# Strassen's products with adding DMAs in the feed-forwards of a two-block model

## The chip, the cores and the metric

The kernel runs on one NeuronCore of a Trainium2 chip. The metric is device time in microseconds; the median of three runs of the kernel before is 2211.48 us (2207.61 to 2212.41). TensorE (PE) multiplies, VectorE (DVE) and ScalarE (ACT) work elementwise, GpSimd (POOL) helps with small things, and SyncE (SP) issues the DMAs.

## What is computed

256 tokens of width 1024 pass through two layers of one block and two of another. Each layer has a feed-forward, a mixer and a second feed-forward, so there are eight feed-forwards of one form, and only these are changed:

```
def swiglu(x, w13, w2):            # x: 256 x 1024, w13: 1024 x 5632, w2: 2816 x 1024
    a, b = jnp.split(x @ w13, 2, axis=-1)
    return (jax.nn.silu(a) * b) @ w2

x = layer_norm(ALPHA * x + 0.5 * swiglu(x, ...), g, b)      # first block
x = x + 0.5 * rms_norm(swiglu(rms_norm(x, g0), ...), g1)    # second block
```

All is float32. The mixers (gated recurrences, attention, convolutions) are as before.

## The kernel before

The tokens are two halves of 128, i = 0 and 1. A product is made of float32r parts: each operand is split into a rounded part (hi, wh, xh) and the rest (lo, wl, xl), and `mm3` (L301) adds hi*hi, hi*lo and lo*hi into PSUM, three matmuls with 512 columns moving for each 128 rows of the weights.

All weights come as one stream of 128x1024 tiles of 512 KB, the units, in the order in which they are used. `fetch` (L226) has SP load them into one of four stages, `split` makes the two parts: ACT copies a half into wh (L267), DVE subtracts it into wl (L273). `run_all` keeps the splits some units ahead of the matmuls (2 to 5), and the fetches four units ahead of the splits (STAGES).

A feed-forward has 11 groups of 256 hidden columns. A group takes four units, whose 512 columns are 256 of a and 256 of b. The first two groups (OWN) are done for each half of the tokens by itself, the others by `joint` for both halves at once: 12 matmuls to a unit, 48 to a group. `hidden` makes silu(a)*b of a group (L400, L402, L405); two steps later it is transposed (L285) and split (L410, L411), and it is then what stands in front of w2: `rows` and `joint` multiply 22 units of w2, each 128 x 1024, into two PSUM banks for each half ("big" in the trace, 12 matmuls for a unit). The table `FFN` gives the order: groups, and between them 8 and 8 units of w2; the last six (LAST) are done by each half for itself. Then comes the norm of that half, whose output `to_x` (L308, L309) transposes and splits into xh and xl.

A scheduler orders PE, ACT and DVE by a cost model; SP and GpSimd keep the order of the program. The code for a stage "s" (PRODUCTS, NEEDS, `operand`) is there but no entry of `FFN` calls it.

Of the kernel before, what the change touches and what calls it, by code (L numbers as in the profile page):

```python
# [19 lines left out]
P = 128  # L20
# [55 lines left out]
class Core:  # L76
# [5 lines left out]
    def __init__(self, ctx, tc, a, out, order):  # L82
        self.tc, self.nc, self.a, self.out = tc, tc.nc, a, out
        self.order = order
        p = lambda n, b, **k: ctx.enter_context(tc.tile_pool(name=n, bufs=b, **k))
        self.cp = p("cp", 1)
        self.stg = p("stg", STAGES)
        self.whp = p("whp", 2 * RING)
        self.sp = p("sp", SLOTS)
        self.vp = p("vp", 2)  # L90
        self.st = p("st", 12)
        self.big = p("big", 4, space=PSUM)
        self.grp = p("grp", 4, space=PSUM)

        self.phase, self.made = [], []
        ffn = _ffn_units()
        for what, _ in order:
            mixer = ("mixer1", 56) if what == "b1" else ("mixer2", 36)
            for kind, made in (("ffn", ffn), (mixer[0], [None] * mixer[1]), ("ffn", ffn)):
                self.phase += [(kind, m) for m in range(len(made))]  # L100
                self.made += made
        self.nunit = len(self.made)
        self.raw, self.next_raw = {}, 0
# [48 lines left out]
    def run_all(self):  # L152
# [3 lines left out]
        def part(i, h):  # L156
            hi, lo = (t[:, i, 512 * h:512 * h + 512] for t in (self.xh, self.xl))
            self.pin(self.nc.scalar.activation(hi, self.xT0[i][h], AF.Copy))
            self.pin(self.nc.vector.tensor_sub(lo, self.xT0[i][h], hi))
# [39 lines left out]
    def lead(self):  # L199


        kind, n = self.phase[min(self.pos[0], self.nunit - 1)]
        left = dict(ffn=len(_ffn_units()), mixer1=56, mixer2=36)[kind] - n
        if self.made[min(self.pos[0] + PAIR, self.nunit - 1)]:
            return PAIR
        return LEAD + (MORE if n < FIRST else max(0, MORE - left // RAMP))

    def paired(self):
        return int(self.made[min(self.next_split, self.nunit - 1)] is not None)
# [5 lines left out]
    def fetch(self, v):  # L215
        while self.next_dma <= min(v, self.nunit - 1):
            made = self.made[self.next_dma]
            if made is None:
                t = self.stages[self.next_dma] = self.stg.tile([P, 1024], F32, tag="stg", name=self.nm("stg"))
            elif made[0] in NEEDS:  # L220
                t = self.raw[NEEDS[made[0]], made[1]] = self.whp.tile([P, 1024], F32, tag="w", name=self.nm("raw"))
            else:
                t = None
            if t is not None:
                for c in (slice(0, 512), slice(512, 1024)) if self.next_raw == 0 else (slice(0, 1024),):
                    self.nc.sync.dma_start(t[:, c], self.a["ws"][self.next_raw][:, c])  # L226
                self.next_raw += 1
            self.next_dma += 1

    def operand(self, p, u):  # L230


        raw, add = self.raw, self.nc.vector.tensor_add
        if p == "p1":
            return raw["11", u]
        if p == "q5":
            t = raw.pop(("11", u))
            add(t, t, raw["12", u])
            raw["t1", u] = t
            return t  # L240
        if p == "p6":
            t = raw["t2", u] = self.whp.tile([P, 1024], F32, tag="w", name=self.nm("sum"))
            add(t, raw.pop(("t1", u)), raw["22", u])
            return t
        if p == "p3":
            return raw["22", u]
        if p == "p7":
            t = raw.pop(("12", u))
            add(t, t, raw.pop(("22", u)))
            return t  # L250
        if p == "p2":
            return raw["21", u]
        t = raw.pop(("t2", u))
        add(t, t, raw.pop(("21", u)))
        return t

    def split(self, u):
        while self.next_split <= min(u, self.nunit - 1):
# [3 lines left out]
            w = self.stages.pop(v) if made is None else self.operand(*made)  # L262
# [3 lines left out]
            for h, c in enumerate(halves if made is None else [slice(0, 1024)]):  # L266
# [8 lines left out]
            self.next_split += 1  # L275
            self.fetch(v + STAGES)
# [26 lines left out]
    def to_x(self, i, srcs):  # L303

        for h, src in enumerate(srcs):
            tp = self.transposed(src)
            hi, lo = (t[:, i, 512 * h:512 * h + 512] for t in (self.xh, self.xl))
            self.nc.scalar.activation(hi, tp, AF.Copy)  # L308
            self.nc.vector.tensor_sub(lo, tp, hi)  # L309

# [15 lines left out]
    def rows(self, i, ks, xT, accs, first, last):  # L326
# [3 lines left out]
        for k in ks:  # L330
# [12 lines left out]
            yield  # L343

# [31 lines left out]
    def ffn(self, i, rs):  # L376
# [8 lines left out]
        J["rs", i] = rs  # L385
        for g in range(OWN):
            yield from self.group(i, lambda acc: self.hidden(J, i, acc, g))
# [29 lines left out]
    def joint(self, J, rs):  # L417

        nc = self.nc
        for what, *at in FFN:  # L420
            if what == "g":
                acc = [self.bank(self.grp, "g") for _ in range(2)]
                for u in range(4):
# [7 lines left out]
                    if u == 3:  # L431
                        for i in range(2):
                            self.hidden(J, i, acc[i], at[0])
                    yield
            else:
                for k in range(*at):
                    wh, wl = self.units[self.pos[1]]
                    for i in range(2):
                        xh, xl = J["h", i, k]
                        self.mm3(J["accs", i], xh, xl, wh, wl, k == 0, False)  # L440
                    self.both(1)
                    yield
        J["done"] = True

# [15 lines left out]
    def ln_residual(self, i, accs, l, n, pre=None):  # L460
# [26 lines left out]
        self.to_x(i, xs)  # L487
# [35 lines left out]
    def rms(self, i, accs, post, pre, fac, spread):  # L523
# [37 lines left out]
        self.to_x(i, xg)  # L561
# [16 lines left out]
    def first_rms(self, i, pre):  # L578
# [6 lines left out]
        self.to_x(i, xg)  # L585
# [764 lines left out]
def _ffn_units():  # L1350

    out = [None] * (4 * OWN)
    for what, *at in FFN:
        if what == "s":
            out += [(p, u) for p in PRODUCTS for u in range(2)]
        else:
            out += [None] * (4 if what == "g" else at[1] - at[0])
    return out + [None] * len(LAST)


def _blocks(w, g):
# [4 lines left out]
    for p in PRODUCTS:  # L1366
        if p in NEEDS:
            r, c = (int(n) - 1 for n in NEEDS[p])
            parts.append(w[r, :, c].reshape(2, 2, P, 512).transpose(0, 2, 1, 3).reshape(2, P, 1024))
# [3 lines left out]
def _ffn(w_in, w_out):  # L1373
    groups, w_out = _pairs(w_in), _rows(w_out)
    parts = [groups[:4 * OWN]]
    for what, *at in FFN:
        if what == "s":
            parts.append(_blocks(w_in, *at))
        else:
            parts.append(groups[4 * at[0]:4 * at[0] + 4] if what == "g" else w_out[at[0]:at[1]])  # L1380
# [96 lines left out]
```

## Time and profile before

| | |
|---|---|
| median of three runs | 2211.48 us |
| profiled execution | 2206.83 us |
| its span | 2205.1 us |
| PE busy | 2169.9 us, 98%, 10256 matmuls |
| DVE, ACT, POOL busy | 66%, 53%, 12% |
| DMA queue of SP | 392.73 MB, 53.8% of 16 engines |
| units loaded (stg) | 711 of 512 KB and 2 of 256 KB |

Busy time of PE counts a matmul from its start to its modelled end, 0.39 us, though the next one starts earlier; the pace is read from the chain of waits, where the pieces of PE follow each other. The DMA share is the busy time of the 16 engines over 16 times the stretch. A line of a helper (L301, L267, L273) collects all stages, so stretches of the feed-forward are looked at by themselves.

### The profile page before, as it was taken

To read this page: it belongs to the slowest core of one execution; us is meant where nothing else is said; L and a number is where in the kernel's file an instruction comes from. 1 tells how busy PE (TensorE), PEld (TensorE's weight loads), DVE (VectorE), ACT (ScalarE), POOL (GpSimd) and SP (SyncE) were. 2 spreads that over 40 slices of the span, in tenths; PEclk is the share of its full clock that TensorE was granted. 3 is DMA by queue.
4 is the path that set the end of the run, shared out by engine and by line. 5 is a ranking of instruction groups with operands and counts; after the bars stand their busy time and mean duration, and the time that the engine had idled before them with its cause. 6 is when DMAs were issued, how large, how long until landed. Compare 5 with 4: busy or idle time off the path is not lost.

```text
span 2205.1 us, 29139 instructions
## 1 busy us (share of the span) xinstructions
PE 2169.9 (98%) x10256; PEld 1791.8 (81%) x10256; DVE 1456.1 (66%) x2653; ACT 1173.5 (53%) x2339; POOL 271.5 (12%) x319
## 2 busy tenths in 40 slices
PE   8999999999999999999999999999999999999998
PEld 6888888888888888888878887788888888788887
DVE  6656787655755679666584668676657466877463
ACT  6544755544544475554554554665446355566352
POOL 0000420000000033001001004610100100650000
PEclk9999999999999999999999999999999999999999
DMA  7855455655565445565645643537555474345561
GB/s 275 271 189 158 148 182 175 223 196 189 182 205 188 156 158 181 180 203 191 210 157 196 218 145 120 172 102 238 182 190 177 157 236 149 114 134 167 177 219 49
DMA packets 115299, 394.59 MB, mean 179 GB/s; under 512 B 12880, under 2 KB 15312, under 8 KB 115152
## 3 DMA queue, kind: packets, MB, share of 16 engines
q1 hardware_dynamic: 115152, 392.73, 53.8%
q8 instruction: 80, 1.31, 0.2%
q14 instruction: 67, 0.55, 0.1%
HBM read 391.63 MB, written 1.05 MB: 178 GB/s over the span
## 4 chain that ended last, share of the span: by engine, by line
PE 88%; DVE 5%; ACT 2%; DMA 2%; POOL 2%; issue 1%; SPq 0%; DVEq 0%; POOLq 0%; ACTq 0%
PE g L301 54%; PE big L301 26%; PE g L285 3%; DMA stg<-in_ws_dram 2%; DVE wl L273 2%; ACT wh L267 1%; PE big L1150 1%; PE big L1179 1%; PE big L680 1%; DVE x L481 0%; DVE t L480 0%; PE big L1097 0%; POOL cu L1023 0%; PE big L882 0%; POOL qk L1024 0%
## 5 line engine op out<-in xcount | busy, mean ns | idle before, releaser
L273 DVE TENSOR_TENSOR wl<-stg,wh 128x512 fp32r<-128x512 f32 x1410 | 952.0, 708 | 506.7 <-ACT wh L267 498.5
L267 ACT ACTIVATE wh<-stg 128x512 fp32r<-128x512 f32 x1424 | 831.5, 625 | 622.7 <-PE g L301 313.6
L301 PE MATMUL g<-wh,xh 128*128 128x512 f32 x1952 | 783.0, 401 | 11.5 <-ACT wh L267 6.9
L301 PE MATMUL g<-wl,xh 128*128 128x512 f32 x1952 | 763.5, 391 | 0.0
L301 PE MATMUL g<-wh,xl 128*128 128x512 f32 x1952 | 762.6, 392 | 0.0
L301 PEld LDWEIGHTS g<-wh,xh 128*128 128x128 f32 x1952 | 368.4, 189 | 89.1 <-ACT xh L308 8.1
L301 PEld LDWEIGHTS g<-wh,xl 128*128 128x128 f32 x1952 | 367.9, 188 | 80.2 <-DVE xl L309 1.4
L301 PEld LDWEIGHTS g<-wl,xh 128*128 128x128 f32 x1952 | 368.6, 189 | 70.9 <-DVE wl L273 0.4
L301 PE MATMUL big<-wh,hT 128*128 128x512 f32 x1408 | 392.1, 391 | 0.0
L301 PEld LDWEIGHTS big<-wh,hT 128*128 128x128 f32 x1408 | 262.6, 188 | 53.6
L301 PE MATMUL big<-wl,hT 128*128 128x512 f32 x704 | 222.3, 390 | 0.0
L301 PEld LDWEIGHTS big<-wl,hT 128*128 128x128 f32 x704 | 132.2, 188 | 27.9
L373 POOL TENSOR_TENSOR m<-m,nhalf 128x1 f32<-128x1 f32 (+1 forms) x24 | 23.1, 964 | 848.3 <-DVE m L372 848.3
L507 POOL TENSOR_TENSOR m<-m,nhalf 128x1 f32<-128x1 f32 x24 | 15.3, 638 | 639.6 <-DVE m L506 639.6
L411 DVE TENSOR_TENSOR hT<-g,hT 128x256 fp32r<-128x256 f32 x176 | 68.2, 419 | 32.6 <-ACT hT L410 32.5
L410 ACT ACTIVATE hT<-g 128x256 fp32r<-128x256 f32 x176 | 59.3, 375 | 54.3 <-PE g L285 53.9
L400 ACT ACTIVATE sg<-g,m 128x256 f32<-128x256 f32 x88 | 41.0, 466 | 87.2 <-PE g L301 87.0
L405 DVE TENSOR_TENSOR sg<-g,sg 128x256 f32<-128x256 f32 x88 | 37.1, 421 | 69.1 <-ACT sg L400 67.0
L400 ACT ACTIVATE sg<-g 128x256 f32<-128x256 f32 x88 | 33.2, 377 | 54.9 <-PE g L301 54.9
L285 PE MATMUL g<-con,sg 128*128 128x128 f32 x352 | 57.4, 273 | 3.4 <-DVE sg L405 2.0
L285 PEld LDWEIGHTS g<-con,sg 128*128 128x128 f32 x352 | 43.7, 140 | 20.6 <-PE g L285 3.7
L402 DVE SCALAR_TENSOR_TENSOR sg<-g,sg 128x256 f32<-128x256 f32 x88 | 37.1, 421 | 30.2 <-ACT sg L400 28.9
(273 smaller groups left out, 1669.6 us busy)
## 6 DMA issues: line engine op xcount, KB each, us to landing
stg<-in_ws_dram SPq DMA_DIRECT2D x711, 512.0 KB, 4.0
row<-in_norm_gain_dram SPq DMA_DIRECT2D x24, 256.0 KB, 5.5
row<-in_ln_g_dram SPq DMA_DIRECT2D x12, 256.0 KB, 5.2
row<-in_ln_b_dram SPq DMA_DIRECT2D x12, 256.0 KB, 6.4
xT<-in_xT_dram SPq DMA_DIRECT2D x4, 256.0 KB, 6.4
x<-in_x_dram SPq DMA_DIRECT2D x4, 256.0 KB, 5.8
out_dram<-x SPq DMA_DIRECT2D x4, 256.0 KB, 2.0
con<-in_con_dram SPq DMA_DIRECT2D x1, 528.0 KB, 6.1
```

Source lines behind the costliest of these rows:

```text
L267: r = self.nc.scalar.activation(hi[:, c], w[:, c], AF.Copy)
L273: self.nc.vector.tensor_sub(lo[:, c], w[:, c], hi[:, c])
L285: self.nc.tensor.transpose(tp[:, hs(j)], src[:, hs(j)], self.ident)
L301: self.nc.tensor.matmul(accs[c], a, b[c], start=start and q == 0, stop=stop and q == 2)
L373: self.nc.gpsimd.tensor_tensor(out, out, self.nhalf[:, 0:n], op=ALU.pow)
L400: nc.scalar.activation(sg[:, 0:256], acc[:, 0:256], AF.Silu, scale=1.0 if rs is None else rs)
L402: nc.vector.scalar_tensor_tensor(sg[:, 256:512], acc[:, 256:512], 0.5, sg[:, 0:256], op0=ALU.mult, op1=ALU.mult)
L405: nc.vector.tensor_mul(sg[:, 256:512], acc[:, 256:512], sg[:, 0:256])
L410: nc.scalar.activation(t[:, 0:256], tp[:, 0:256], AF.Copy)
L411: nc.vector.tensor_sub(t[:, 256:512], tp[:, 0:256], t[:, 0:256])
L680: nc.tensor.matmul(ps[:, 64 * h:64 * h + 64].rearrange("p (c m) -> p c m", m=m), Z[:, hs(h)], view(Z[:, hs(h)], m)[:, :, 1, :], start=True ...
L1150: nc.tensor.matmul(ps[:, hh * S + j * P:hh * S + j * P + P], J["aq", i][r, hs(head // 2)], J["ak", j][r, hs(head // 2)], start=True, stop= ...
```

## The change

Of the 11 groups of a feed-forward, the first two stay with each half, group 10 is joint as before, and the other eight become four pairs of two groups ("s" in `FFN`). A pair is a product of 2x2 blocks: the activations X as token halves (rows) by halves of the 1024 features (columns), the weights as halves of the 1024 rows by 512 columns of a and 512 of b. Seven products p1, p2, q5, p3, p6, p7, q4 of one block with one block take the place of eight; each is 12 matmuls, from two units. Four of the products need sums of weight blocks, three need sums of blocks of X.

The sums of X are made once for a feed-forward by `sums` on DVE and ACT, for which `to_x` keeps an unrounded copy. The sums of weights are made in place: SP loads blocks 11, 21 and 22 into buffers of the ring that also holds the split parts; when a block is split, `added` has GpSimd issue a DMA that adds the next block out of DRAM to the same buffer. So the buffer of p1 becomes that of q5, p6 and q4 in turn, and that of p3 becomes p7's. Splits of these units are one ACT and one DVE instruction of 1024 columns. `pair` lets products accumulate in two PSUM banks, copies what it needs of a partial sum to SBUF by ACT (`keep`), and puts one unit of w2 (`on`) after each of the products in GAPS. Splits run five units ahead (PAIR) near products.

```
-FFN = (("g", 2), ("g", 3), ("r", 0, 8), ("g", 4), ("g", 5), ("g", 6), ("g", 7), ("r", 8, 16),
-       ("g", 8), ("g", 9), ("g", 10))
-LAST = (16, 17, 18, 19, 20, 21)
-PRODUCTS = ("p1", "q5", "p6", "p3", "p7", "p2", "q4")
-NEEDS = dict(p1="11", q5="12", p6="22", p2="21")
+FFN = (("g", 10), ("s", 2, 0, 1, 2, 3), ("s", 4, 20, 21, 4, 5), ("s", 6, 6, 7, 8, 9), ("s", 8, 10, 11, 12),
+       ("r", 13))
+LAST = (14, 15, 16, 17, 18, 19)
+PRODUCTS = ("p1", "p2", "q5", "p3", "p6", "p7", "q4")
+LOADS = dict(p1="11", p2="21", p3="22")
+ADDS = dict(q5=("p1", "12"), p6=("q5", "22"), q4=("p6", "21"), p7=("p3", "12"))
+BLOCKS = ("11", "21", "12", "22")
+GAPS = ("p1", "q5", "p6", "p7")
...
+            elif made[0] in LOADS:
+                t = self.raw[made[:2]] = self.whp.tile([P, 1024], F32, tag="w", name=self.nm("raw"))
+                self.nc.sync.dma_start(t, self.block(LOADS[made[0]], *made[1:]))
...
+    def added(self, p, u, base):
+        t = self.raw.pop((p, u))
+        for q, (of, b) in ADDS.items():
+            if of == p:
+                self.nc.gpsimd.dma_start(t, self.block(b, u, base), accum_op=ALU.add)
+                self.raw[q, u] = t
...
             self.next_split += 1
+            if product:
+                self.added(*made)
             self.fetch(v + STAGES)
...
+        if keep:
+            for h, tp in enumerate(tps):
+                t = self.sh["A", i, h] = self.slot(name="A")
+                self.nc.scalar.activation(t, tp, AF.Copy)
...
+    def sums(self, X):
...
+        def parts(p, t):
+            hi, lo = self.slot((P, 512), F32R, "Xh"), self.slot((P, 512), F32R, "Xl")
+            nc.scalar.activation(hi, t, AF.Copy)
+            nc.vector.tensor_sub(lo, t, hi)
+            X[p] = hi, lo
+        nc.vector.tensor_sub(a22, a22, a21)
+        nc.vector.tensor_sub(a21, a11, a21)
+        yield 1
+        parts("q5", a22)
+        yield 1
+        minus(a11, a22, a11)
+        yield 1
+        minus(a12, a11, a12)
...
+    def pair(self, J, g, ks):
+        first = dict(p1="p1", p2="p2", q5="q5", p3="q5", p6="p1", p7="p1", q4="p1")
...
+        def after(p):
+            if p in ("p1", "q5", "p6", "p7"):
+                keep(p)
+            if p == "p2":
+                t = sg[0] = kept.pop("p1")
+                add(t, bank[p])
+                silu(t, t, 0)
+            elif p == "p6":
+                t = kept.pop("p6")
+                add(t, bank["p3"])
+                hidden(0, t, sg.pop(0))
+            elif p == "p7":
+                add(kept["p7"], kept.pop("q5"))
+            elif p == "q4":
+                t = self.slot(name="sg")
+                silu(t, bank[p], 1)
+                hidden(1, kept.pop("p7"), t)
+        for p in PRODUCTS:
+            bank[p] = self.bank(self.grp, "g") if first[p] == p else bank[first[p]]
+            xh, xl = J["X"][p]
+            for u in range(2):
+                wh, wl = self.units[self.pos[1]]
+                for j in range(2):
+                    k = 2 * u + j
+                    for q, (x, w) in enumerate(((xh, wh), (xh, wl), (xl, wh))):
+                        nc.tensor.matmul(bank[p], x[:, hs(k)], w[j], start=first[p] == p and k + q == 0,
+                                         stop=k == 3 and q == 2, skip_group_check=True)
...
+                if u:
+                    after(p)
+                yield
+            if p in rows:
+                yield from self.on(J, rows[p])
```

ACT in the first feed-forward, joint groups, before: wh are the splits of one unit each from its stage, sg the silu of a group, hT the transposed hidden part.

```order
L267 ACTIVATE wh_239_1162<-stg_221_1070 128x512
L400 ACTIVATE sg_186_927<-g_170_839 128x256
L267 ACTIVATE wh_239_1162<-stg_221_1070 128x512
L267 ACTIVATE wh_242_1182<-stg_224_1090 128x512
L410 ACTIVATE hT_194_955<-g_193_952 128x256
L410 ACTIVATE hT_196_961<-g_195_958 128x256
L267 ACTIVATE wh_242_1182<-stg_224_1090 128x512
L267 ACTIVATE wh_245_1202<-stg_227_1110 128x512 x2
```

ACT now, in the second pair of the first feed-forward: raw_148 and raw_151 are the two buffers that p1, q5, p6 and q4 share, raw_180 and raw_185 those of p3 and p7; kp1, kq5, kp6 are the kept partial sums.

```order
L259 ACTIVATE wh_195_838<-raw_180_773 128x1024
L259 ACTIVATE wh_199_852<-raw_185_789 128x1024
L259 ACTIVATE wh_201_865<-raw_148_639 128x1024
L259 ACTIVATE wh_204_877<-raw_151_659 128x1024
L501 ACTIVATE kp1_192_818<-kp1_192_818 128x512
L259 ACTIVATE wh_208_904<-stg_197_843 128x512
L494 ACTIVATE kq5_207_890<-g_203_870 128x512
L259 ACTIVATE wh_208_904<-stg_197_843 128x512
L259 ACTIVATE wh_210_910<-raw_180_773 128x1024
L259 ACTIVATE wh_212_920<-raw_185_789 128x1024
L259 ACTIVATE wh_215_938<-stg_206_882 128x512 x2
L259 ACTIVATE wh_218_946<-raw_148_639 128x1024
```

Splits of product units (L259 from raw) stand in one row with the copies of partial sums; the copy kp6 of this pair comes two rows behind the last one shown, after the second split of q4.

GpSimd up to its first norm, before: nothing of it belongs to the weights.

```order
L1311 MEMSET nhalf_81 128x4
L1264 MEMSET one256_87 4x256
L1260 CAST mask_82<-mask_91_441 128x448
L373 ISA
L373 TENSOR_TENSOR m_354_1717<-m_354_1717,nhalf_81 128x1
```

GpSimd now, from the second pair's first adds on: each row is one adding DMA into a raw buffer.

```order
L245 DMA raw_148_639<-in_ws_dram 128x1024
L245 DMA raw_151_659<-in_ws_dram 128x1024
L245 DMA raw_148_639<-in_ws_dram 128x1024
L245 DMA raw_151_659<-in_ws_dram 128x1024
L245 DMA raw_180_773<-in_ws_dram 128x1024
L245 DMA raw_185_789<-in_ws_dram 128x1024
L245 DMA raw_148_639<-in_ws_dram 128x1024
L245 DMA raw_151_659<-in_ws_dram 128x1024
```

These eight adds of a pair stand in the order in which their splits do; the pair's six loads stay with SP.

## Rows read from the trace of the kernel before

**Rows 1.** The page: span, busy time of each engine, granted clock, chain by engine.

```profile
span 2205.1 us, 29139 instructions
PE 2169.9 (98%) x10256; PEld 1791.8 (81%) x10256; DVE 1456.1 (66%) x2653; ACT 1173.5 (53%) x2339; POOL 271.5 (12%) x319
...
PEclk9999999999999999999999999999999999999999
...
PE 88%; DVE 5%; ACT 2%; DMA 2%; POOL 2%; issue 1%; SPq 0%; DVEq 0%; POOLq 0%; ACTq 0%
```

**Rows 2.** Chain through one feed-forward: start us, us, engine and line.

```profile
401.45 4.80 DMA stg<-in_ws_dram
...
408.60 10.94 PE g L301 x48
419.54 0.44 PE g L285 x4
419.98 8.21 PE g L301 x36
428.19 2.72 PE big L301 x12
430.91 0.44 PE g L285 x4
431.35 19.10 PE big L301 x84
...
551.35 1.36 PE big L301 x6
```

**Rows 3.** Timeline, one unit's split on ACT and DVE: start us, us, engine.

```profile
640.64 1.15 ACT L267 ACTIVATE wh<-stg 128x512 fp32r<-128x512 f32 x2 [1.79 <-PE g L301]
...
641.30 1.30 DVE L273 TENSOR_TENSOR wl<-stg,wh 128x512 fp32r<-128x512 f32 x2 [1.65 <-ACT wh L267]
```

**Rows 4.** Stretches: us, busy us of each engine, clock, DMA share, GB/s.

```profile
core 0: us, PE busy (x) PEld busy (x) DVE busy (x) ACT busy (x) POOL busy (x), PEclk, DMA share, GB/s
480.00:560.00 80.00, 79.93 (x362) 65.95 (x362) 42.57 (x75) 37.37 (x74) 0.00 (x0) 1.00 0.57 187
65.00:70.00 5.00, 5.00 (x24) 4.14 (x23) 1.10 (x2) 1.62 (x3) 0.00 (x0) 1.00 1.00 395
```

**Rows 5.** Groups of instructions: shapes and count, busy us, mean ns, idle before.

```profile
L309 DVE TENSOR_TENSOR xl<-g,xh 128x512 fp32r<-128x512 f32 x44 | 28.4, 685 | 1.5 <-ACT xh L308 1.5
L308 ACT ACTIVATE xh<-g 128x512 fp32r<-128x512 f32 x44 | 24.1, 595 | 23.7 <-PE g L285 23.6
L544 DVE SCALAR_TENSOR_TENSOR x<-r,m,x 128x512 f32<-128x512 f32 x24 | 17.7, 746 | 1.3 <-POOL m L507 1.3
```

**Rows 6.** The page's DMA queue, and issues: count, KB, us to landing.

```profile
q1 hardware_dynamic: 115152, 392.73, 53.8%
...
stg<-in_ws_dram SPq DMA_DIRECT2D x711, 512.0 KB, 4.0
...
row<-in_ln_g_dram SPq DMA_DIRECT2D x12, 256.0 KB, 5.2
row<-in_ln_b_dram SPq DMA_DIRECT2D x12, 256.0 KB, 6.4
```

**Rows 7.** DVE's splits from 480 to 560 us, then from 220 to 300 us.

```profile
L273 DVE TENSOR_TENSOR wl<-stg,wh 128x512 fp32r<-128x512 f32 x55 | 36.3, 689 | 33.5 <-ACT wh L267 33.5
...
L273 DVE TENSOR_TENSOR wl<-stg,wh 128x512 fp32r<-128x512 f32 x40 | 31.0, 800 | 7.8 <-ACT wh L267 7.8
```

**Rows 8.** Waits in all: us, times, longest.

```profile
ACT wh L267 <- DMA stg<-in_ws_dram: 65.8, 64, 4.8
```

More of the change, by code (lines that the diff above doesn't have):

```diff
@@ L261, in split @@
             made = self.made[v]
-            w = self.stages.pop(v) if made is None else self.operand(*made)
+            product = self.product(v)
+            w = self.raw[made[:2]] if product else self.stages.pop(v)
             hi = self.whp.tile([P, 1024], F32R, tag="w", name=self.nm("wh"))
@@ L265, in split @@
             halves = [slice(0, 512), slice(512, 1024)]
-            for h, c in enumerate(halves if made is None else [slice(0, 1024)]):
+            for h, c in enumerate([slice(0, 1024)] if product else halves):
                 r = self.nc.scalar.activation(hi[:, c], w[:, c], AF.Copy)
@@ L301, in mm3, with to_x @@
                 self.nc.tensor.matmul(accs[c], a, b[c], start=start and q == 0, stop=stop and q == 2)
[L303 removed]
+    def to_x(self, i, srcs, keep=False):
+        tps = []
         for h, src in enumerate(srcs):
@@ L385, in ffn @@
         J["rs", i] = rs
+        if i == 1:
+            J["X"] = {}
+            self.later(2, lambda: self.start(self.sums(J["X"])))
         for g in range(OWN):
@@ L417, in joint @@
     def joint(self, J, rs):
-        nc = self.nc
-        for what, *at in FFN:
-            if what == "g":
+        for what, n, *ks in FFN:
+            if what == "s":
+                yield from self.pair(J, n, ks)
+            elif what == "g":
                 acc = [self.bank(self.grp, "g") for _ in range(2)]
@@ L432, in joint @@
                         for i in range(2):
-                            self.hidden(J, i, acc[i], at[0])
+                            self.hidden(J, i, acc[i], n)
                     yield
             else:
[L436 to L442, printed above, removed]
@@ L443, in joint, with on, keep, add @@
-        J["done"] = True
+                yield from self.on(J, n)
+        J["done"] = True
+    def on(self, J, k):
+        wh, wl = self.units[self.pos[1]]
+        for i in range(2):
+            xh, xl = J["h", i, k]
+            self.mm3(J["accs", i], xh, xl, wh, wl, k == 0, False)
+        self.both(1)
+        yield
+    def pair(self, J, g, ks):
+        nc = self.nc
+        first = dict(p1="p1", p2="p2", q5="q5", p3="q5", p6="p1", p7="p1", q4="p1")
+        bank, kept, sg = {}, {}, {}
+        rows = dict(zip(GAPS[len(GAPS) - len(ks):], ks))
+        def keep(p):
+            t = kept[p] = self.slot(name="k" + p)
+            nc.scalar.activation(t, bank[p], AF.Copy)
+        def add(t, other):
+            nc.vector.tensor_add(t, t, other)
+        def silu(out, src, i):
+            rs = J["rs", i]
+            nc.scalar.activation(out, src, AF.Silu, scale=1.0 if rs is None else rs)
+        def hidden(i, t, sg):
+            nc.vector.scalar_tensor_tensor(t, t, -0.5 if J["rs", i] is None else -1.0, sg,
+                                           op0=ALU.mult, op1=ALU.mult)
+            def turn():
+                hi, lo = self.to_T(t, "hT")
+                for c in range(4):
+                    J["h", i, 2 * g + c] = hi[:, hs(c)], lo[:, hs(c)]
+            self.later(2, turn)
+        def after(p):
[19 more added lines that the diff above has]
+            for u in range(2):
+                wh, wl = self.units[self.pos[1]]
+                for j in range(2):
[3 more added lines that the diff above has]
+                                         stop=k == 3 and q == 2, skip_group_check=True)
+                for i in range(2):
+                    self.pos[i] += 1
+                if u:
+                    after(p)
+                yield
+            if p in rows:
+                yield from self.on(J, rows[p])
@@ L1375, in _ffn @@
     parts = [groups[:4 * OWN]]
-    for what, *at in FFN:
+    for what, n, *ks in FFN:
         if what == "s":
-            parts.append(_blocks(w_in, *at))
+            parts += [_blocks(w_in, n), w_out[list(ks)]]
         else:
-            parts.append(groups[4 * at[0]:4 * at[0] + 4] if what == "g" else w_out[at[0]:at[1]])
+            parts.append(groups[4 * n:4 * n + 4] if what == "g" else w_out[n:n + 1])
     return parts + [w_out[list(LAST)]]
```

98 lines of the change are left out of this document (47 added, 51 removed).

## The prediction

> **What bounds the kernel now.** I began with the page's engine row and its chain [rows 1]. TensorE is busy for 2169.9 of 2205.1 us and stands on 88% of the chain that ended last, with the granted clock at its upper level (2.4 GHz) in every slice. DVE follows with 66%, ACT with 53%. So the kernel ends when its matmuls end, and taking matmuls away is worth their full pace for as long as nothing else takes the place of TensorE.
>
> The pace comes from the chain through one feed-forward [rows 2]: 84 matmuls of 512 columns in 19.10 us, 48 in 10.94 us, that is 0.2275 us each. Twelve of them (one unit of w_out, both token halves) take 2.73 us, four small transposes 0.44 us. Nothing but TensorE stands on that stretch for 140 us. The one gap ahead of it is a load: DMA for 4.80 us, then a split. The reader should see that a feed-forward is a straight line of PE pieces, each unit fed by one 512 KB load, two ACT copies and two DVE subtractions that all lie beside it.
>
> Then the helpers, because they are what the change loads. A unit's two halves take ACT 1.15 us and DVE 1.30 us [rows 3]. In a stretch of feed-forward DVE is busy 42.57 of 80 us, ACT 37.37, GpSimd not at all, and the 16 DMA engines have a share of 0.57 while they move 187 GB/s [rows 4]. That is the number to keep: 0.57 of all engines for one load per 2.73 us, so a 512 KB load costs 0.57 x 524288 B / 187 GB/s = 1.60 us of all 16 engines. In a crowded stretch they are fuller and faster: share 1.00 at 395 GB/s, 1.33 us a load [rows 4]. I take the middle, 1.45 us.
>
> **The change part by part.**
>
> *Matmuls.* Two groups cost 2 x 2 x 24 = 96 matmuls, seven products of 12 cost 84. Four pairs save 48 in each feed-forward, 384 in eight, 384 x 0.2275 = 87.3 us. Transposes stay as many (two of four for a pair, where four of two were). Against the profiled execution of 2206.8 us (span 2205.1) TensorE alone would end at 2119.5 us. The median of the runs shown is 2211.5, 4.7 above the profiled one; I add that at the end.
>
> What was one stretch of 8 groups and 15 w_out units (131.8 us: 384 + 180 matmuls and 3.5 us of transposes) becomes four pairs with their 15 w_out units: 336 + 180 matmuls and 3.5 us, 120.9 us; a pair with four rows is 84 x 0.2275 + 4 x 2.73 + 0.88 = 30.9 us (33.6 before).
>
> *Splits.* A product unit is as wide as any other (128x1024) but feeds 6 matmuls, 1.37 us, instead of 12. So a pair needs 14 + 4 splits instead of 8 + 4. DVE: 18 x 1.30, three sums at 0.685, two subtractions for the transposed halves at 0.685, two products at 0.746 (nearest rows, [rows 5]) = 28.3 of 30.9 us. ACT: 18 x 1.15, and four copies out of PSUM, two for the transposes and two silus at 0.595 [rows 5] = 25.5 us. Both fit, DVE with 8% to spare (before, the splits of a pair with its rows took 12 x 1.30 = 15.6). That one 1024-wide instruction replaces two of 512 can only shorten this, so I cost it at the pair's time.
>
> *Sums of the activations.* Per feed-forward seven DVE instructions (5 us) and three ACT copies, behind the first own group, where half of DVE is free [rows 4]: nothing. Without that cover, 5 us x 8 = 40 us. The copies in to_x stand behind those that TensorE waits for: nothing, uncovered 8 x 4 x 0.595 = 19 us, part of the range.
>
> *Loads and adds.* A pair loaded 8 units; now SP loads 6 (three of four blocks, two halves each), and GpSimd issues 8 adding DMAs of 512 KB. All share the 16 engines, for which the page's queue row counts one share [rows 6]. No row shows an adding DMA. Below, it is a plain load: 1.33 us of the engines and 4.0 us to landing [rows 6]. Above, it moves two loads, since the old value must be read out of SBUF as the new one is from HBM: 2 x 1.60 = 3.20 us and 8.0 us, with the issue on GpSimd on top. A gain is excluded: it has to move at least what a load moves. I take two loads at 1.45, 2.90 us, because the engines' time goes with the bytes that they handle, and each byte of the sum is handled twice. The Trainium skill says the same more sharply ("Collectives: The Full Stack", section "The bandwidth ceiling: the fold count and why AG ≠ RS ≠ AR"): a reduce needs two source reads on one ring, which measured half the rate of a copy. No run here shows it yet; by it the sum stays as it is, by a plain load it is the first rival.
>
> So in the stretch of four pairs the engines have 24 + 15 = 39 loads and 32 adds: 39 x 1.45 + 32 x 2.90 = 149.4 us of work against 120.9 us of TensorE. **The DMA engines become the bound there.** What softens it is the distance: splits run five units ahead, and fetches four more, nine units at 120.9 / 71 = 1.70 us, 15.3 us; one load and one split (4.0 + 1.15 + 1.30) must remain, so about 9 us are absorbed in each feed-forward, whose ends are lightly loaded. Stall: 149.4 - 120.9 - 9 = 19.5 us, in eight 156 us.
>
> *Sum:* 2206.8 - 87.3 + 156 = 2275.5, with the 4.7 us to the median **2280 us**, slower by 3.1%. From the ends of the price: loads 1.33, adds 2.66 give 137.0, a stall of 7.1 and 2181 us; loads 1.60, adds 3.20 give 164.8, a stall of 34.9 and 2403 us.
>
> *The new wait.* The split of q5 waits for an add that waits for the split of p1, and so p6 for q5 and q4 for p6. ACT is in order: behind a late q5 split stand the second half of q5, the next rows' splits, and the copies (kp6, kp7) that free a PSUM bank for p7 and q4. PE then waits with them. With an add's latency L (from DVE's end to landing) a pair takes at least 3 x (L + 1.15 + 1.30) and the two splits of q4 (2.6): 3L + 10. At L = 4.0 that is 22 us, hidden by 30.9; at 8.0 it is 34. Break-even with TensorE is L = 7.0.
>
> **The rivals.**
>
> *A: an add costs a plain load.* For it: engines were at 0.57 in a stage, and a burst shows that they can move twice that. Against: two reads. Then 71 x 1.45 = 103 us lie under 120.9, L stays near 4 to 6, and TensorE is the bound with DVE at 92%: I leave 3 us of waits in each feed-forward (less than the 4.80 us that one starved start costs today [rows 2]). 2206.8 - 87.3 + 24 + 4.7 = 2148 us, faster.
>
> *B: VectorE becomes the bound.* Its 512-wide split takes 689 ns in a feed-forward where GpSimd rests and 800 ns in a stretch of the mixer where GpSimd works [rows 7]. If issuing adds did the same, DVE would need 18 x 1.30 x 1.16 + 4.9 = 32.0 us a pair, 1.1 over TensorE, 35 us in all: 2206.8 - 87.3 + 35 + 24 + 4.7 = 2183 us. Against it: those GpSimd instructions read tiles, an issue does not. The Trainium skill ("SBUF — State Buffer", section "Who interferes with whom") has this rule: a VectorE instruction with two SBUF inputs contends with a GpSimd instruction that reads SBUF, not with one that only writes. By it this rival falls away; the trace agrees as far as its readers go (800 against 689 ns).
>
> *C: latency, not bandwidth, slower by more.* GpSimd issues the adds in order and the first of each two holds up the second. If issue and queueing bring L to 10 us (an 8 us transfer and 2 us ahead of it), a pair takes 40 us; four pairs lose 4 x 9.1 - 9 = 27 us, eight times 219 us: 2206.8 - 87.3 + 219 + 4.7 = 2343 us. It decides from L = 7 on and loses against before from about 8.5. For it: under load the small row loads already land after 5.2 to 6.4 us [rows 6]. Against: each add has five units (8.2 us) until its sum is due.
>
> **How the numbers follow.** Adds at two loads, DMA-bound: 0.46, of which 0.04 end faster, 0.05 within, 0.37 slower (its own range is 2181 to 2403). A: 0.29, faster. B: 0.08, of which 0.07 faster and 0.01 within. C: 0.17, slower. Within means 0.2%, some 4 us, which is about what this measurement can tell from no change. So faster 0.40, same 0.06, slower 0.54. The range is 2145 to 2390: it takes in most of A and ends where a tenth of the slow cases lies beyond.
>
> **What would show it.** Right: DMA share near 1.0 through the pairs, ACT's copies of raw waiting for DMAs by more than 100 us in total (64 waits of 65.8 us in all before, [rows 8]), PE idle ahead of the q5, p6 and q4 products, pairs of 34 us or more, and adds that take about twice a load's engine time. The matmul part is right if PE has 384 matmuls fewer at the same 0.2275 us. A shows as a share of 0.85 or less and pairs of 31 us; B as splits of 128x1024 above 1.5 us with DVE never idle; C as a DMA share well below 1 while ACT waits for adds that take 7 us or more to land. The sign is wrong if adds of 512 KB hold the engines for less than 2.63 us: then 56.6 + 32 x 2.63 = 140.8 us, and the stall is the 10.9 us that TensorE saves in a feed-forward.

## The result, and the profile after

The changed kernel takes 2414.76 us (median of 4; 2411.20 to 2422.18) against 2210.47 of the kernel before (median of 4): a ratio of 1.093, 95% interval 1.0901 to 1.0958. The prediction, 2280 us (2145 to 2390), had the sign right and missed the size: it is 135 us too low, and the time lies above the range. The profiled execution took 2414.87 us.

The page of the kernel after answers to [rows 1, 6]: span, busy engines, granted clock by slice, DMA queues, chain by engine, issues with the median us to landing.

```profile
span 2413.1 us, 28933 instructions
PE 2175.0 (90%) x9872; PEld 1765.3 (73%) x9872; DVE 1752.8 (73%) x2621; ACT 1405.2 (58%) x2335; POOL 492.4 (20%) x575
...
PEclk9889999989999999998899999999989989999999
...
q1 hardware_dynamic: 105936, 359.18, 42.5%
q0 software_dynamic: 36864, 134.23, 29.8%
...
PE 29%; DMA 12%; issue 6%; DVE 3%; POOL 3%; ACT 1%; POOLq 0%; DVEq 0%; ACTq 0%
...
stg<-in_ws_dram SPq DMA_DIRECT2D x455, 512.0 KB, 4.7
raw<-in_ws_dram POOLq DMA_DIRECT2D x256, 512.0 KB, 8.2
raw<-in_ws_dram SPq DMA_DIRECT2D x192, 512.0 KB, 6.4
```

384 matmuls are gone. PE is at 90% where it was at 98%. The chain can be followed back over 54% of the span only (its shares add up to that, from about 1110 us on); of this part PE has 29 of 54, a bit over half, where it had 88% before, and waiting for DMAs has 12 of 54. The queue of the adds, q0, takes 29.8% of the engines: 0.298 x 2413.1 / 256 = 2.81 us of all 16 engines for an add. A plain 512 KB load costs 0.425 x 2413.1 x 0.524 / 359.18 = 1.50 us. The clock is no longer at its upper level in every slice.

The waits of the kernel after (total us, times, longest), the first of them beside [rows 8]:

```profile
ACT wh L259 <- DMA raw<-in_ws_dram: 362.3, 166, 7.2
...
PE g L540 <- ACT kp L494: 70.1, 26, 7.6
PE g L279 <- DVE kp L504: 66.4, 28, 6.7
...
PE g L540 <- ACT kq L494: 57.9, 15, 8.3
```

PE hardly waits for the weights themselves. It waits for ACT's copies of partial sums (L494) and for DVE's last product ahead of the transposes (L504). Both stand in their engine's row behind a split whose data is late. By product, PE stands at the first matmul of p3 (57.9 us, the kq row), of q4 (44.5) and of p7 (25.6), not ahead of q5 and p6 as the prediction had said: it is the copies, not the split weights, that come too late.

A stretch here is what lies between the first and the last matmul of the products of one feed-forward. Its mean over the eight is 156.8 us, where TensorE alone needs 121; outside, the kernel takes 2414.8 - 8 x 156.8 = 1160 us, and 2206.8 - 8 x 131.8 = 1152 before, with the 131.8 us that the prediction worked out for the same part. So nearly all of the loss is in the pairs. In a stretch the stops of PE longer than the pace take 27.8 us and matmuls at the lower clock 6.9 us (summed over its matmuls from the trace). The stretch of the third feed-forward, columns as in [rows 4]:

```profile
663.20:819.30 156.10, 131.89 (x548) 105.53 (x548) 103.69 (x125) 91.69 (x130) 24.07 (x28) 0.92 0.90 240
```

The DMA engines are at 0.90, not at 1.0; over the eight stretches it is 0.88 to 0.93. The pairs are not alike: from its first matmul to the next pair's, the first pair takes 30.9 to 31.0 us in the second to fourth feed-forwards, TensorE's own time, and the two behind it 41 to 55 us. The timeline of the seventh feed-forward shows one stop from its cause to its end:

```profile
1942.66 1.63 POOL L624 TENSOR_TENSOR xg<-x,row 128x512 f32<-128x512 f32 x1
1942.92 5.63 DVE L265 TENSOR_TENSOR wl<-stg,wh 128x512 fp32r<-128x512 f32 x1
1943.91 1.62 POOL L626 TENSOR_TENSOR gg<-row,row 128x512 f32<-128x512 f32 x1
...
1950.22 0.88 POOL L245 DMA_DIRECT2D raw<-in_ws_dram  x1 [2.23 <-issue]
...
1956.99 1.06 ACT L259 ACTIVATE wh<-raw 128x1024 fp32r<-128x1024 f32 x1 [7.21 <-DMA raw<-in_ws_dram]
...
1958.57 0.58 ACT L494 ACTIVATE kq<-g 128x512 f32<-128x512 f32 x1
1959.20 0.80 PE L540 MATMUL g<-wh,Xh 128*128 128x512 f32 x1 [8.26 <-ACT kq L494]
```

GpSimd multiplies gains of the next norm (four instructions in a row), and meanwhile one subtraction of DVE takes 5.63 us instead of 0.69. The next add is issued at 1950.22. It lands at 1956.91. The split of its sum holds ACT until 1956.99, the copy kq stands behind it, and PE waits 8.26 us. What follows on PE, 12 matmuls in 5 us and then 45 in 10 us:

```profile
1959.20:1964.20 5.00, 5.00 (x12) 3.95 (x13) 3.15 (x5) 3.16 (x4) 0.00 (x0) 0.50 1.06 205
1964.60:1974.60 10.00, 9.66 (x45) 7.71 (x44) 7.18 (x8) 5.78 (x7) 1.74 (x2) 1.00 0.67 190
```

After the stop the granted clock is 0.50 (1.2 GHz), and a matmul takes 0.427 us instead of 0.2275. In the whole kernel 307 matmuls go at that pace, 61 us lost.

### The profile page after: what moved, and what is told of

The parts are those of the page before. It is cut to its first block, busy times and chain, and to the rows that moved or that the text cites. A ratio compares the mean times of both kernels' runs of the same rounds, so it can differ in the third digit from the quotient of the medians.

```text
span 2413.1 us, 28933 instructions
## 1 busy us (share of the span) xinstructions
PE 2175.0 (90%) x9872; PEld 1765.3 (73%) x9872; DVE 1752.8 (73%) x2621; ACT 1405.2 (58%) x2335; POOL 492.4 (20%) x575
## 3 DMA queue, kind: packets, MB, share of 16 engines
q1 hardware_dynamic: 105936, 359.18, 42.5%
q0 software_dynamic: 36864, 134.23, 29.8%
## 4 chain that ended last, share of the span: by engine, by line
PE 29%; DMA 12%; issue 6%; DVE 3%; POOL 3%; ACT 1%; POOLq 0%; DVEq 0%; ACTq 0%
DMA raw<-in_ws_dram 12%; PE g L295 10%; PE big L295 8%; PE g L540 6%; DVE wl L265 2%; PE g L279 2%; ACT wh L259 1%; PE big L1255 1%; POOL raw L245 1%; PE big L1284 1%; POOL xg L624 1%; POOL cu L1128 0%; PE big L1202 0%; PE big L1168 0%; PE big L1174 0%
## 5 line engine op out<-in xcount | busy, mean ns | idle before, releaser
L265 DVE TENSOR_TENSOR wl<-raw,wh 128x1024 fp32r<-128x1024 f32 x448 | 540.5, 1222 | 350.9 <-ACT wh L259 348.8
L259 ACT ACTIVATE wh<-raw 128x1024 fp32r<-128x1024 f32 x448 | 466.6, 1056 | 434.0 <-DMA raw<-in_ws_dram 362.3
L265 DVE TENSOR_TENSOR wl<-stg,wh 128x512 fp32r<-128x512 f32 x898 | 634.5, 739 | 116.5 <-ACT wh L259 110.8
L259 ACT ACTIVATE wh<-stg 128x512 fp32r<-128x512 f32 x912 | 527.7, 623 | 212.0 <-PE big L295 82.8
L245 POOL DMA_DIRECT2D raw<-in_ws_dram x256 | 222.6, 870 | 990.5 <-DVE wl L265 760.9
L295 PE MATMUL g<-wh,xh 128*128 128x512 f32 x928 | 380.4, 410 | 12.0 <-ACT wh L259 6.9
L295 PE MATMUL g<-wl,xh 128*128 128x512 f32 x928 | 366.5, 395 | 6.9 <-POOL wl L263 6.9
L295 PE MATMUL g<-wh,xl 128*128 128x512 f32 x928 | 364.8, 396 | 0.0
L540 PE MATMUL g<-wh,Xh 128*128 128x512 f32 x512 | 219.7, 429 | 83.5 <-ACT kq L494 57.9
L540 PE MATMUL g<-wl,Xh 128*128 128x512 f32 x512 | 214.7, 419 | 0.0
L540 PE MATMUL g<-wh,xh 128*128 128x512 f32 x384 | 163.6, 426 | 44.5 <-ACT kp L494 44.5
L540 PE MATMUL g<-wl,xh 128*128 128x512 f32 x384 | 160.4, 418 | 0.0
L540 PE MATMUL g<-wh,xl 128*128 128x512 f32 x384 | 160.0, 417 | 0.0
```

The lines of the kernel that those rows point to most:

```text
L245: self.nc.gpsimd.dma_start(t, self.block(b, u, base), accum_op=ALU.add)
L259: r = self.nc.scalar.activation(hi[:, c], w[:, c], AF.Copy)
L265: self.nc.vector.tensor_sub(lo[:, c], w[:, c], hi[:, c])
L295: self.nc.tensor.matmul(accs[c], a, b[c], start=start and q == 0, stop=stop and q == 2)
L540: nc.tensor.matmul(bank[p], x[:, hs(k)], w[j], start=first[p] == p and k + q == 0, stop=k == 3 and q == 2, skip_group_check=True)
```

## The experiments

Edits are against the changed kernel; ratios are to the kernel before, with 95% intervals.

**1. Plain loads in place of the adds (e1_plain).** The sums are left out.

```
-self.nc.gpsimd.dma_start(t, self.block(b, u, base), accum_op=ALU.add)
+self.nc.gpsimd.dma_start(t, self.block(b, u, base))
```

> The adding DMAs become plain loads into the same buffers, issued from GpSimd at the same places with the same waits (the weight sums are not made: part of the computation is left out). Bytes theory (the 16 DMA engines' work per feed-forward, 39 loads x 1.50 us + 32 adds x 2.81 us = 148 us, is the bound): the work falls to 71 x 1.5 = 106 us, under TensorE's 121 us, and the time to 2150-2190 us. Chain theory (three adds in series per pair at 8.2 us from issue to landing, with ACT in order behind them): a plain load lands after 5 to 6.5 us, a pair's chain is 25 to 30 us, and the time falls to 2160-2220 us with stops left at kq and kp. Clock theory (stops make the clock fall): slow-paced matmuls disappear with the stops.

2217.6 us, 1.0038 (1.0022 to 1.0054): inside the chain theory's range, above that of the bytes. The same queue, with the same packets and bytes:

```profile
q0 software_dynamic: 36864, 134.23, 17.0%
```

That is 0.170 x 2216.0 / 256 = 1.47 us of the engines for each, against 2.81 with the add. The mean stretch is 132.4 us. So 197 of the 204 us go with the adding itself. But it is not the 2148 us of rival A: some 11 us a stretch stay. In the fourth to seventh feed-forwards a third pair takes 42 to 45 us; from the timeline of one of these:

```profile
1776.88 1.31 POOL L624 TENSOR_TENSOR xg<-x,row 128x512 f32<-128x512 f32 x1
1777.16 5.32 DVE L265 TENSOR_TENSOR wl<-stg,wh 128x512 fp32r<-128x512 f32 x1
...
1791.84 0.80 PE L540 MATMUL g<-wh,Xh 128*128 128x512 f32 x1 [6.61 <-ACT kq L494]
```

The gains hold up DVE here too, with no adding DMA anywhere.

**2. The same adds, into two spare tiles that nothing waits for (e2_traffic).** The sums are left out; small copies on DVE and GpSimd keep each issue behind its split.

```
-SLOTS = 31
+SLOTS = 28
-self.nc.gpsimd.dma_start(t, self.block(b, u, base), accum_op=ALU.add)
+self.nc.vector.tensor_copy(self.tiny[:, c], lo[:, 0:1])
+self.nc.gpsimd.tensor_copy(self.seen[:, c], self.tiny[:, c])
+self.nc.gpsimd.dma_start(self.spare[self.next_spare % 2], self.block(b, u, base), accum_op=ALU.add)
... (the tiles tiny, seen and spare are made at the start)
```

> The same 256 adds with the same bytes, issued after the same splits, go into two spare tiles that nothing reads (sums left out; slots 28 instead of 31 to make room). No split waits for an add any more. Bytes theory: the engines' work stays at 148 us per feed-forward and so most of the loss: 2280-2400 us, with waits now on the plain loads. Chain theory: without the wait the time is TensorE's, 2140-2190 us.

2298.95 us, 1.0409 (1.0388 to 1.0430): in the bytes theory's range, and the chain theory missed. So each of the two runs misses one of the simple theories. The fifth feed-forward's stretch:

```profile
1222.70:1361.70 139.00, 127.77 (x549) 102.90 (x548) 110.63 (x151) 92.58 (x130) 47.12 (x62) 0.95 1.00 275
```

Here the DMA engines are full (1.00; 0.98 to 1.03 over the eight), and the mean stretch, 139.6 us, is the 149.4 - 9 = 140.4 us that the prediction worked out from bytes. The bound was real and well sized, its lead too: 7.0 us of the adds' engine time in a feed-forward lie ahead of its first product (summed from the packets). In the changed kernel the stretch is 17.2 us longer than that, 138 us in eight: what waiting for the adds costs on top. That the forecast was 135 us too low is nearly the same number, though this run also loses some 20 us outside the stretches (run 7).

**3. An own PSUM bank for p3 (e3_p3bank).**

```
-first = dict(p1="p1", p2="p2", q5="q5", p3="q5", p6="p1", p7="p1", q4="p1")
+first = dict(p1="p1", p2="p2", q5="q5", p3="p3", p6="p1", p7="p1", q4="p1")
...
+                add(t, kept["q5"])
```

> p3 gets a PSUM bank of its own, so it does not wait for ACT's copy of q5, which stands behind the waiting split of p6 in ACT's order; one more sum on DVE per pair (0.69 us). Same adds, same bytes, same result. Bytes theory: no change, 2400-2430 us. Order theory (the copies behind a late split hold TensorE): the kq stops go, some 2.7 us in three of four pairs, 60 to 90 us less: 2320-2360 us.

2425.66 us, 1.0983 (1.0959 to 1.1007): no faster, so the order theory's 2320 to 2360 us missed. Its longest waits of PE:

```profile
PE g L541 <- ACT kp L494: 150.4, 30, 13.3
PE g L279 <- DVE kp L504: 63.0, 34, 4.8
```

The stops at kq vanish and come back at kp (70.1 us before the edit), 119.0 us of them at the first matmul of p7. No single copy is the cause; the next one in the row is as late.

**4. Two pairs, plain groups between them (e4_two).**

```
+FFN = (("g", 10), ("s", 2, 0, 1, 2, 3), ("g", 6), ("g", 7), ("s", 4, 20, 21, 4, 5), ("g", 8), ("g", 9),
+       ("r", 6), ("r", 7), ("r", 8), ("r", 9), ("r", 10), ("r", 11), ("r", 12), ("r", 13))
```

> Two pairs per feed-forward instead of four, with two plain groups between them and two behind, and eight w_out units after that; the result is the same. Engine work per feed-forward: 48 loads x 1.5 + 16 adds x 2.81 = 117 us under 140 us of TensorE. Bytes theory: the distance recovers between the pairs, each pair takes 30.9 us, and 24 x 8 = 192 matmuls of 0.2275 us are saved, 44 us: about 2170 us, faster than before. Chain theory: each pair is late by what its chain exceeds 30.9 us (3 x 8.5 + 10 = 35.5), less the distance of 9 us that each pair starts with again: also 2170-2190 us.

2282.33 us, 1.0338 (1.0321 to 1.0355): both theories missed. TensorE's sum is 2167 us (192 matmuls fewer); 115 us are lost, with engines that have time to spare in the second feed-forward's stretch:

```profile
428.80:526.90 98.10, 88.42 (x384) 71.56 (x383) 66.61 (x93) 58.73 (x96) 10.33 (x12) 0.97 0.86 244
```

The prediction's own 3L + 10 comes near. Adds land 8.7 us after their issue starts (the page counts from there, so GpSimd's 0.87 us are in it), and 0.3 us lie between DVE's end and that start: L = 9.0, and a pair needs 37.0 us against 30.9; 16 pairs would lose 98 us. The chain theory had let the lead absorb that.

**5. Two pairs, adds not waited for (e9_two_traffic: 2 and 4 together).** The sums are left out.

> Two pairs with one w_out unit in a gap, as in the run with two pairs (2282 us), but the same adds go into two spare tiles and no split waits for them (the sums are left out; 28 slots instead of 31). If what two pairs lost is the adds waited for in series, it is gone: TensorE's 2167 us, some stops and the cost that fewer slots had outside the pairs with four pairs (22 us) make 2170 to 2205 us. If it is the engines' time, 14 loads x 1.50 + 8 adds x 2.75 us and no relief from the lightly loaded groups between the pairs, the time stays at 2260 to 2290 us.

2267.87 us, 1.0264 (1.0230 to 1.0297). I expected the stall to go, and most of it stayed; the time lies in the range that was given for the engines' work, but the next run speaks against that. These rows show another reason; from the timeline of its first feed-forward:

```profile
123.86 2.38 ACT L263 ACTIVATE wh<-stg 128x512 fp32r<-128x512 f32 x4 [3.62 <-DMA stg<-in_ws_dram]
124.52 0.69 DVE L269 TENSOR_TENSOR wl<-stg,wh 128x512 fp32r<-128x512 f32 x1 [3.56 <-ACT wh L263]
125.13 0.69 DVE L508 SCALAR_TENSOR_TENSOR kp<-kp,kp 128x512 f32<-128x512 f32 x1
...
125.96 0.63 PE L283 MATMUL g<-con,kp 128*128 128x128 f32 x4 [3.64 <-DVE kp L508]
```

A plain load is late between the adds. Its unit is not due on PE for several units, but ACT stands at its split, DVE at that split's subtraction, and behind it is the product whose transposes PE has reached. **The lead protects the weights; it doesn't protect the copies and products in the same in-order rows.**

**6. The same, transposes four units behind their product (e15_traffic_turn).** The sums are left out.

```
-            self.later(2, turn)
+            self.later(4, turn)
```

> Two pairs whose adds go to spare tiles and are not waited for (2268 us, sums left out), with the transposes four units behind their product instead of two. TensorE waited 49.8 us there in 14 stops. In-order copies: these stops go and the clock's falls with them, 2205 to 2235 us. Bytes as such: the engines' work has not changed, 2255 to 2270 us.

2237.99 us, 1.0130 (1.0113 to 1.0146): 30 us back with the same adds, 3 us above the range of in-order copies and 17 below that of the bytes. In the second and third feed-forwards the two pairs and their groups take 85.6 and 85.7 us, with at most 0.3 us of stops: late loads are then fully covered, though the DMA engines are at 0.95. The second:

```profile
423.20:508.80 85.60, 85.41 (x384) 69.54 (x383) 65.60 (x102) 58.48 (x94) 16.20 (x24) 1.00 0.95 271
```

What is left sits mostly in the fifth to seventh (95.5 to 98.9 us), where gains are multiplied, and outside the stretches. There the bytes alone thus cost two pairs nothing; the order in the rows did.

**7. The kernel before with fewer slots (e14_slots)**, to read 2, 5 and 6.

```
-SLOTS = 31
+SLOTS = 28
```

> The kernel before with 28 slots instead of 31, nothing else. The two traffic runs, which had 28, lost some 21 us outside the pairs. If the slots did it, 2220 to 2235 us; if not, 2208 to 2216 us.

2216.64 us, 1.0031 (1.0021 to 1.0040), between the two ranges: 7 us of the 21 that these runs lost outside the stretches; the rest, perhaps their small copies, was not tried.

**8. Adds of an eighth (e5_small).** The other columns of the sums are left out.

```
-self.nc.gpsimd.dma_start(t, self.block(b, u, base), accum_op=ALU.add)
+self.nc.gpsimd.dma_start(t[:, 0:128], self.block(b, u, base)[:, 0:128], accum_op=ALU.add)
```

> Each adding DMA adds only the first 128 of the 1024 columns (the other columns of the sums are left out), with its issue, its waits and its place as in the changed kernel. Bytes: 56.6 us of loads and some 10 us of adds lie far under TensorE's 121 us, so no stall remains, 2120 to 2150 us. Chain: a pair takes three times the time from an add's issue to its landing, plus 10 us; if a small add lands after about 4 us, that is 22 us, under the 30.9 us of the matmuls, and only the pairs in which GpSimd multiplies gains lose something (6 feed-forwards, some 8 us each): 2150 to 2180 us. If landing stays at 8 us whatever the bytes, the latency is a fixed price of an adding DMA: 34 to 37 us a pair, 2240 us or more, with the clock falling as well.

2180.6 us, 0.9863 (0.9847 to 0.9879), at the edge of what the series predicts. The adds land after 3.1 us, so 3 x 3.4 + 10 = 20 us, and most pairs take 30.7 to 32.3 us, but 41.3, 38.3, 40.2 and 40.2 us as the third pair of the fourth to seventh feed-forwards, where the gains are. An adding DMA has no large fixed delay (3.1 us against 8.2); its bytes make it late.

**9. Gains behind the adds (e6_late).**

```
-                ahead(60, (l, 5), pre)
+                ahead(90, (l, 5), pre)
```
and alike at the two other calls.

> The changed kernel with GpSimd's multiplications of the gains moved behind all 32 adds of a feed-forward. If they hold up the subtractions of the splits and the adds queued behind them, the third pair of four feed-forwards and the second of two get 5 to 12 us shorter and TensorE's clock falls there less often: 2350 to 2385 us instead of 2415. If bytes and the chain alone make the loss, the time stays at 2405 to 2420 us.

2379.62 us, 1.0785 (1.0757 to 1.0813): 35 us less, as expected. The third pairs of the fifth to seventh feed-forwards fall from 51.9, 52.9 and 50.5 us to 35.3, 38.0 and 35.0; the fourth pairs, into which the gains move, grow by 3 to 7 us.

**10. Transposes later in the changed kernel (e12_turn: the edit of 6, three units behind the last pair), and with the gains late (e13_turn_late).**

> The changed kernel with the transposes of a pair's results four units behind their last product instead of two (three behind the last pair). If the lead is lost because copies that TensorE needs soon stand in ScalarE's queue behind splits of late data, most of the 66 us that TensorE waited there for VectorE's last product goes: 2345 to 2385 us against 2415. If the DMA engines' work or the three adds in series set the end of a pair, the wait comes back at the next product: 2400 to 2420 us.

> The same, and GpSimd's gains behind all 32 adds (alone 2380 us). If the two causes are separate, both savings add up: 2305 to 2355 us. If they are one, it is no faster than the better of the two, 2345 to 2380 us.

2404.13 us, 1.0873 (1.0846 to 1.0899), and 2364.44 us, 1.0702 (1.0686 to 1.0718). The first is a miss: only 11 us come back. PE's waits in it:

```profile
PE g L540 <- ACT kp L494: 72.8, 26, 6.7
PE g L279 <- DVE kp L504: 56.5, 28, 7.1
PE g L540 <- ACT kq L494: 56.1, 15, 6.9
```

Those for kp and kq are as they were, and even the transposes, moved away, lose only 10 us of their wait. So with four pairs on end the place of the transposes doesn't set the pace; the expectation gave this to the engines' work or the series of adds, and the run doesn't tell these two apart. The second lies above its range too, but the two edits add up: 11 + 35 against 50 us.

**11. Wide gaps: two pairs with two w_out units in each gap (e7_gaps), and with the gains behind all adds (e8_gaps_late).**

```
+FFN = (("g", 10), ("g", 9), ("s", 2, 0, 1, 2, 3, 20, 21, 18, 19), ("g", 6), ("g", 7), ("g", 8),
+       ("s", 4, 4, 5, 6, 7, 12, 13, 14, 15))
+LAST = (16, 17, 8, 9, 10, 11)
... (and two units from the list in each gap)
```

> Two pairs in each feed-forward instead of four, with two w_out units in each of the four gaps between products instead of one, 192 matmuls fewer than before (43.7 us). A pair then lasts 84 x 0.2275 + 8 x 2.73 + 0.9 = 41.8 us. Chain: three adds in series need 3 x 9 + 10 = 37 us, less than the pair, so nothing waits but where GpSimd's gains come between: 2165 to 2185 us, faster than the kernel before (2210). Bytes: a pair's 14 loads and 8 adds hold the engines for 14 x 1.50 + 8 x 2.75 = 43 us against 41.8: some 2 us lost a pair, 2190 us; both are under the 2282 us of two pairs with one unit in a gap. If each pair costs a fixed stall by being there, as with two pairs and narrow gaps: 2270 to 2290 us.

> The same two wide pairs, with GpSimd's multiplications of the gains behind all 16 adds of a feed-forward. If wide gaps cover the chain, this is the fastest: TensorE's sum is 2210 - 43.7 = 2167 us, and I expect 2163 to 2175 us. If the gains do no harm in wide gaps, it is within 3 us of the kernel with wide gaps alone. If every pair costs a fixed stall: 2260 us or more.

2199.63 us, 0.9952 (0.9940 to 0.9964), and 2231.27 us, 1.0084 (1.0069 to 1.0100). With the same adds as run 4, the wide pairs are 83 us faster, and 0.5% faster than before; 2165 to 2190 us was expected. A second pair takes 42.0 us in nearly every feed-forward, TensorE's own 41.8; that of the fifth:

```profile
1262.00:1303.90 41.90, 41.84 (x188) 34.25 (x187) 33.10 (x48) 29.89 (x50) 3.42 (x4) 1.00 0.90 263
```

PE is busy throughout, the clock at 1.00, the DMA engines at 0.90. Adds land after 8.5 us, so a pair longer than 3 x 8.8 + 10 = 36 us hides them. The first pairs of the first four feed-forwards still take 46 to 52 us; in each of these PE stops once for 2.7 to 4.0 us at the transposes behind L504. The late gains are a miss: they now fall into the second pair, right behind its last add, and in the whole kernel PE waits 34.4 us (9 times) for L504 instead of 15.9 (7 times).

**12. Wide gaps, one plain group behind the second pair, transposes four units later, gains between the adds of the two pairs (e10_turn).**

```
+FFN = (("g", 10), ("g", 9), ("s", 2, 0, 1, 2, 3, 20, 21, 18, 19), ("g", 6), ("g", 7),
+       ("s", 4, 4, 5, 6, 7, 12, 13, 14, 15), ("g", 8))
+LAST = (8, 9, 10, 11, 16, 17)
...
-            self.later(2, turn)
+            self.later(4, turn)
...
-                ahead(60, (l, 5), pre)
+                ahead(48, (l, 5), pre)
```

> The two wide pairs (2199.6 us) with one of the plain groups moved behind the second pair, so that the transposes of a pair's result can stand four units behind it instead of two, and with GpSimd's gains issued between the two pairs. If what was left of the loss is TensorE waiting at those transposes for VectorE's last product (15.9 us in 7 stops) with the clock's falls behind them, the time is 2172 to 2188 us. If the same copies are late wherever the transposes stand, it stays within 5 us of 2199.6.

2187.62 us, **0.9884 (0.9868 to 0.9901)**: the best complete version, 1.2% faster than before and 9% faster than the change as made. What each of its edits is worth was not separated. Its two longest waits of PE:

```profile
PE g L279 <- DVE kp L504: 10.0, 7, 2.4
PE g L295 <- ACT wh L259: 7.0, 2, 5.5
```

**13. Three pairs with gaps of six, six and four units (e11_three).**

```
+FFN = (("g", 10), ("s", 2, 0, 1, 2, 3, 20, 21), ("g", 9), ("s", 4, 4, 5, 6, 7, 18, 19), ("g", 8),
+       ("s", 6, 8, 9, 10, 11))
+LAST = (16, 17, 12, 13, 14, 15)
... (and one or two units from the list in each gap)
```

> Three pairs in each feed-forward, six w_out units in the gaps of the first two and four in those of the third, a plain group between the pairs, gains behind the second pair; 288 matmuls fewer than before, TensorE's sum 2210 - 65.5 = 2145 us. A pair with six rows lasts 36.4 us against 37 us of the chain: nearly covered; one with four rows 30.9 us, losing 6 us. Chain: 8 x (6 + 1 + 1) = 64 us and a clock loss of some 15 us: 2215 to 2235 us. Bytes: 12 loads x 1.50 + 8 adds x 2.75 = 40 us in a pair of 36.4 us, relieved by the group between the pairs: 2150 to 2185 us.

2279.59 us, 1.0310 (1.0295 to 1.0325): both theories too low. Adds land after 9.0 us, so L = 9.3 and a pair needs 37.9 us against 36.4 and 30.9: (1.5 + 1.5 + 7.0) x 8 = 80 us of the 135 lost. 142 matmuls go at the lower clock, 28 us more; the rest is not shown.

## Why the prediction was wrong

*What bounds the kernel, and the matmuls:* right. 384 fewer, same pace at the upper clock. The saving is real where little waits: e10_turn keeps 25 of the 44 us that its 192 matmuls are worth.

*Price of an add:* right. 2.81 us against 2.90, a load 1.50 against 1.45, and 1.47 from the adds' own queue (run 1). The Trainium skill's rule that a reduce reads two sources ("Collectives: The Full Stack", section "The bandwidth ceiling: the fold count and why AG ≠ RS ≠ AR") agrees with this price, and so do the packets: 0.328 us for 4 KB in an add, 0.159 in a load (medians). Rival A's price is refuted.

*Stretch by bytes:* the size was right where only bytes act (139.6 us measured, 140.4 predicted). For the kernel as it is, the working stopped too early.

*The step that failed:* "Stall: 149.4 - 120.9 - 9 = 19.5 us" has no term for "The new wait". I set bandwidth and the series of adds against each other, as likeliest case and rival C, and gave either the lead. They act together: waiting for adds leaves the engines idle (0.88 to 0.93 in place of 1.00), so the bound by bytes is passed by 17.2 us a feed-forward, 138 us. And "about 9 us are absorbed" held for the bytes (run 2) but not for the waits: ACT and DVE are in order, so a late split delays the copies that PE needs at once, which runs 5 and 6 show for two pairs. The prediction said "PE then waits with them" and then credited 9 us all the same.

The sizes do not close. Rival C without its credit is, at L = 10, 219 + 72 = 291 us and 2415 us, the time that was measured; that is luck. L, from DVE's end to landing, is 0.3 + 8.2 = 8.5 us, which gives 32 x (35.5 - 30.9) = 147 us. Of the other 144 us of the 291 lost against TensorE's 2124, two parts were not priced: the lower clock after stops (61 us), and the gains (35 us, part of it clock). At least some 50 us have no run that tells their cause, and how all of these overlap with the bytes is not settled: each was measured by taking it away alone or in pairs.

*Rival B:* the mechanism was half seen. A split of 128x1024 takes 1222 ns, so VectorE is not the bound. But I only looked at adds being issued, and the gains come between the pairs' splits: the Trainium skill's rule ("SBUF — State Buffer", section "Who interferes with whom") that a VectorE instruction with two SBUF inputs contends with a GpSimd one that reads SBUF agrees with the 5.63 us of a 0.69 us subtraction. Averaged, [rows 7] had made that 800 against 689 ns.

*Sums of X, copies in to_x:* next to nothing, as forecast: outside the stretches the kernel changed by 8 us.

## What to carry to other kernels

A queue's lead covers only what is fetched ahead: look for copies and products that another engine needs at once behind an instruction that may wait for a DMA, and don't count on the lead for those. A series of DMAs that depend on each other is priced as its whole length against the stretch that holds it, with landing times as under load. Where bytes and such a series are both near the bound, neither alone gives the time; make the stretch longer than the series, as with two wide pairs, before adding more of them. Where TensorE starts to stop, price its lower clock behind the stops as well.

## What the runs showed of the hardware

- A 512 KB DMA that adds into SBUF holds the 16 engines for 2.81 us and lands 7.9 to 9.1 us after its issue starts (medians of the runs); with 64 KB it lands after 3.1 us (e5_small), a plain 512 KB load from the same queue after 5.0 (e1_plain). Issuing one takes GpSimd 0.87 us, a plain one 0.54.
- Four GpSimd instructions of 1.3 to 1.6 us on end held one DVE subtraction for 5.3 us (e1_plain) and 5.63 us (after): not slowed by a share, but until 0.56 us after the last of them had ended, where the subtraction alone takes 0.69.
- After stops of a few us the granted clock is 0.50. It was so for 215 us in the changed kernel, 188 of them in the pairs' stretches, and for 15 us in the kernel before.
